# S5 and pooling layer on one core: pooled sums held until the scan is done, pooled maps spread over four output steps, S5 parameters computed among the first channel tiles

## The chip, the cores and the metric

The kernel runs on one core of a Trainium2 chip. The core has a matrix engine (TensorE, PE in the rows; its weight loads are PEld), a vector engine (VectorE, DVE), an activation engine (ScalarE, ACT), a general engine (GpSimd, POOL) and a queue engine that mostly issues transfers (SyncE, SP). Times are device microseconds (us) of one launch; the metric is the median of the runs. The change is called faster or slower by comparing medians of interleaved runs of both kernels.

## The reference

One layer of a diffusion backbone for 128 prompt tokens and 512 sample tokens, width 1024. The part that the change touches is the token mixer:

```
z = h @ w_in + b_in                    # 1024 -> 1024 (u_a) + 512 (u_b) + 2 x 1024 (gates)
s[t] = lam_bar * s[t-1] + b_bar u_a[t] # complex, 64 groups x 64 states, forward and backward
y = Re(C s) + D u_a                    # both directions summed
v = gelu(y); v = v * sigmoid(v @ w_glu + b_glu); ya = v @ w_proj_a
pooled = mean over a window of 2, 4, 8 or 16 tokens (four groups of 128 channels) - u_b
yb = (pooled @ w_pool[group]) * pool_scale @ w_proj_b
out = (sigmoid(g_a) * ya + sigmoid(g_b) * yb) @ w_out + b_out
```

Layer norms with modulation stand before it and after it, and a squared-ReLU MLP of width 4096 follows. Everything is float32; a product of two float32 matrices is made of three passes over parts that are split into a rounded high part and the rest (`split`: ScalarE writes the high part, VectorE the low part).

## The kernel before

Channels lie on the 128 partitions, the 640 tokens along the free axis, in two segments of 320. A weight tile is 128 x 1024 (`wsplit`, L324: one transfer on the SP queue, ACT cast at L321, DVE subtraction at L322); `next_w` (L375) keeps two of them ready ahead of use. The kernel is written as a list of steps; a scheduler fixes, when the kernel is built, the order of instructions on each engine from priorities that follow this list, and semaphores between the engines are all that decides at run time.

- 0 to 60 us: layer norm and modulation (`shift_scale`, L286), the transposed input `hf` (L393 and L394) in eight tiles k, its split `hk` (L396 and L397), and the first two tiles of the input projection (`pu0`, `pu1`) that run along with k. Ahead of the loop over k stands `s5_params(*s5_angles())`: some 80 small VectorE instructions that turn the S5 parameters into tables (`pwt`, `pws`, `pqt`, `pqs`, and the scan's factors `lmr`, `lmi`).
- 60 to 170 us: the other six tiles of u_a (`ua_evac`), and for 16 sets of groups the input matrices of the scan (`gen_in`, `in_proj`), which multiply the tables with `wt` and transpose them on TensorE (L466).
- 170 to 300 us: the scan (`scan_step`, L488): 63 steps of the loop, each of four VectorE instructions (L501 to L504) on 128 x 128, in a chain. Every fourth step a `fill(1)` puts one more tile of the input projection on TensorE (`plain`, L586; the 20 fillers are the pooled branch's input and the gates; 16 of them run before the output steps, 48 matmuls each).
- 255 to 310 us on GpSimd: the pooled sums (`pool_mix`, L654), four groups: a memset of a padded tile `ub` (L656), its transfers (L658), the inverse window counts `ic` (L660), window sums by repeated adds (L667), multiplication and subtraction (L671 and L672). The result is `pls[gi]`.
- 300 to 427 us: 16 output steps e. `out_proj(e)` makes 48 matmuls from the scan's states (`psy`, L574 and L577) and its result goes to DRAM (`yd`, L582) by an ACT copy (L579) and two DVE adds. Beside it, in the steps named at the loop's end (L733 to L746), stand: half a filler tile (`halves`, L596), `pool_map(gi)` (L676: splits `pls[gi]` into `ph`, 6 matmuls, ACT scale, split into `ybx`), `pool_proj(m)` (L687: 24 matmuls on the four `ybx`), and `gelu(m)` (L697: loads `yn` back from `yd`, ACT gelu, split into `vx`).
- from 427 us: the GLU (matmuls on `vx`), the projections, the output projection and the MLP. The change does not touch them.

Of the kernel before, what the change touches and what calls it, by code (L numbers as in the profile page):

```python
# [23 lines left out]
NC = NT // TC  # L24
CP = 16
G = 64
# [12 lines left out]
def hybrid_kernel(ctx: ExitStack, tc: tile.TileContext, xin, cc, w_ada0, w_ada, w_in, w_glu, w_pa, w_pool, w_pb,  # L39
# [35 lines left out]
    def bank(name="ax"):  # L75
        return pp[0].tile([P, 512], F32, tag="ax", bufs=axn[0], name=nm(name))
# [80 lines left out]
    def s5_params(s5t, lr, li, mag, r):  # L157

        pw, tmp = [big0[:, 1280 + 1152 * i:2432 + 1152 * i].rearrange("p (a g k) -> p a g k", a=2, k=9) for i in range(2)]

        def cmul(o, a, b, n):
            ab = [a[i].broadcast_to([P, G, n]) for i in range(2)]
            t0, t1 = tmp[:, 0, :, 0:n], tmp[:, 1, :, 0:n]
            V.tensor_tensor(t0, ab[0], b[0], op=ALU.mult)
            V.tensor_tensor(t1, ab[1], b[1], op=ALU.mult)
            V.tensor_tensor(o[0], t0, t1, op=ALU.subtract)
            V.tensor_tensor(t0, ab[0], b[1], op=ALU.mult)
            V.tensor_tensor(t1, ab[1], b[0], op=ALU.mult)
            V.tensor_tensor(o[1], t0, t1, op=ALU.add)

        nc.gpsimd.memset(pw[:, 0, :, 0:1], 1.0)
        nc.gpsimd.memset(pw[:, 1, :, 0:1], 0.0)
        V.tensor_tensor(pw[:, 0, :, 1], mag, r[:, 0], op=ALU.mult)
        V.tensor_tensor(pw[:, 1, :, 1], mag, r[:, 1], op=ALU.mult)

        def pwr(a, b):
            return [pw[:, i, :, a:b] for i in range(2)]

        cmul(pwr(2, 3), pwr(1, 2), pwr(1, 2), 1)
        cmul(pwr(3, 5), pwr(2, 3), pwr(1, 3), 2)  # L180
        cmul(pwr(5, 9), pwr(4, 5), pwr(1, 5), 4)
        for i in range(2):
            S.copy(lmr[:, i], pw[:, 0, :, 8])
        S.mul(lmi[:, 0], pw[:, 1, :, 8], -1.0)
        S.copy(lmi[:, 1], pw[:, 1, :, 8])
        S.copy(pqt[0:64], pw[0:64, :, :, 1:9])
        S.copy(pqt[64:128], pw[64:128, :, :, 8:0:-1])

        den, dn2, lm1 = s5t([P, G]), s5t([P, G]), s5t([P, G])
        V.tensor_tensor(den, lr, lr, op=ALU.mult)  # L190
        V.tensor_tensor(dn2, li, li, op=ALU.mult)
        V.tensor_tensor(den, den, dn2, op=ALU.add)
        V.reciprocal(den, den)
        V.tensor_scalar(lm1, pw[:, 0, :, 1], -1.0, None, op0=ALU.add)
        cf = half([P, 2, G, 1], "cf")
        a, b = s5t([P, G]), s5t([P, G])
        V.tensor_tensor(a, lm1, lr, op=ALU.mult)
        V.tensor_tensor(b, pw[:, 1, :, 1], li, op=ALU.mult)
        V.tensor_tensor(a, a, b, op=ALU.add)
        V.tensor_tensor(cf[:, 0, :, 0], a, den, op=ALU.mult)  # L200
        V.tensor_tensor(a, pw[:, 1, :, 1], lr, op=ALU.mult)
        V.tensor_tensor(b, lm1, li, op=ALU.mult)
        V.tensor_tensor(a, a, b, op=ALU.subtract)
        V.tensor_tensor(cf[:, 1, :, 0], a, den, op=ALU.mult)
        pc = mat4([P, 2, G, 8], "pc")
        cmul([pc[:, 0], pc[:, 1]], [cf[:, 0], cf[:, 1]], pwr(0, 8), 8)
        S.copy(pwt[0:64], pc[0:64])
        S.copy(pwt[64:128], pc[64:128, :, :, ::-1])
        V.tensor_tensor(pws, pwt[:, 0], pwt[:, 1], op=ALU.add)
        V.tensor_tensor(pqs, pqt[:, 0], pqt[:, 1], op=ALU.add)  # L210
# [75 lines left out]
    def shift_scale(q):  # L286

        ps = bank("psa")
        for k2 in range(4):
            for kk in range(2):  # L290
                for g in range(4):
                    T.matmul(ps[32 * g:32 * g + 32, 0:P], sc[:, 2 * k2 + kk, :], wss[q][k2][:, kk, g, :],
                             start=(k2 + kk == 0), stop=(k2 + kk == 4), skip_group_check=True)
        row = half([P, P], "row")
        S.copy(row, ps[:, 0:P])
        pc = bank("psc")
        T.transpose(pc[:, 0:P], row, ident)
        src = pc[:, 0:P].rearrange("p (m f r) -> p m f r", m=2, f=2)
        for mod in range(2):
            b = colt[:, C_BADA + mod * KT + 2 * q:C_BADA + mod * KT + 2 * q + 2].unsqueeze(2).broadcast_to([P, 2, 2])  # L300
            V.scalar_tensor_tensor(modc[:, mod, 2 * q:2 * q + 2, :], src[:, mod, :, 0:2], float(mod), b,
                                   op0=ALU.add, op1=ALU.add)
# [45 lines left out]
    def tv(t):  # L348
        return t.rearrange("p (n c) -> p n c", n=2)
# [32 lines left out]
    hl0, hl1 = wsplit(w_in[0]), wsplit(w_in[1])  # L382
    wss += [shift_scale_load(q) for q in (1, 2, 3)]
    shift_scale(0)
    s5_params(*s5_angles())
    pu0, pu1 = bank2(), bank2()
    for k in range(KT):
        pa, pb = bank("pst"), bank("pst")
        for t in range(1, NTT):
            T.transpose(pa[:, (t - 1) * P:t * P], xs[t][:, k * P:(k + 1) * P], ident)  # L390
        T.transpose(pb[:, 0:P], xs[0][:, k * P:(k + 1) * P], ident)
        hf = half([P, NT], "hf")
        S.activation(hf[:, P:NT], pa, AF.Identity, scale=modc[:, 1, k, 0:1], bias=modc[:, 0, k, 0:1])  # L393
        S.activation(hf[:, 0:P], pb[:, 0:P], AF.Identity, scale=modc[:, 1, k, 1:2], bias=modc[:, 0, k, 1:2])  # L394
        hk = hslot([P, 2, NT], F32R, "hk")
        V.tensor_copy(hk[:, 0, :], hf)  # L396
        V.tensor_tensor(hk[:, 1, :], hf, hk[:, 0, :].bitcast(F32), op=ALU.subtract)  # L397
        hx.append(hk)
        if k % 2:
            if k < KT - 1:  # L400
                shift_scale(k // 2 + 1)
            for hl, pu in ((hl0, pu0), (hl1, pu1)):
                for kk in (k - 1, k):
                    mm_k(pu, hl, hx[kk], kk, KT, SEG)
# [7 lines left out]
    def state(n):  # L412
        return zt[:, n // 2, :, :, n % 2]
# [237 lines left out]
    E = nc.gpsimd  # L651
    ybx, npp = [], [0]

    def pool_mix(gi):  # L654
        u = pool3([P, 784], "ub")
        E.memset(u, 0.0)  # L656
        for uv, dv in zip(segs_of(u), flat_of(ubd[gi])):
            nc.gpsimd.dma_start(uv, dv)  # L658
        ic = pool2([P, NT], "ic")
        nc.gpsimd.dma_start(ic, invc[gi:gi + 1, :].broadcast_to([P, NT]))  # L660
        yield
        s, lo, hi = u, 0, 784
        for lv in range(gi + 1):
            n = pool3([P, 784], "us")
            d0, d1 = ((1, 0), (1, 1), (2, 2), (4, 4))[lv]
            a, b_ = lo + d0, hi - d1
            E.tensor_tensor(n[:, a:b_], s[:, a - d0:b_ - d0], s[:, a + d1:b_ + d1], op=ALU.add)  # L667
            s, lo, hi = n, a, b_
        p = ic
        for sv, uv, iv in zip(segs_of(s), segs_of(u), flat_of(ic)):  # L670
            E.tensor_tensor(iv, sv, iv, op=ALU.mult)  # L671
            E.tensor_tensor(iv, iv, uv, op=ALU.subtract)  # L672
        pls.append(p)
        yield

    def pool_map(gi, p, wph):  # L676
        ph = hslot([P, 2, NT], F32R, "ph")
        split(p, ph[:, 0, :], ph[:, 1, :])
        ps = bank2()
        mm_k(ps, wph[:, :, gi * P:(gi + 1) * P], ph, 0, 1, SEG)  # L680
        f = gt([P, NT], "yb")
        S.activation(tv(f), v2(ps), AF.Identity, scale=colt[:, C_PSC + gi:C_PSC + gi + 1])
        yb = hslot([P, 2, NT], F32R, "ybx")
        split(f, yb[:, 0, :], yb[:, 1, :])
        ybx.append(yb)
# [20 lines left out]
    for s in range(NC - CP - 1):  # L706
        scan_step(s)
        if s == CP - 1:
            last = s5p.tile([P, 2, 2, G], F32, tag="ta", bufs=2, name="last")[:, 0]
            S.copy(last, state(CP))  # L710
            dma(nstate, last)
            S.copy(state(CP), s0t)
        if s % 11 == 3 and s < 50:
            gen_t(3 + s // 11)
            if s < 40:
                gen_q(4 + s // 11)
        if s % 4 == 0 and s < 60:
            fill(1)
    genctx.close()
    mixctx = ctx.enter_context(ExitStack())  # L720
# [5 lines left out]
    wph = wsplit(w_pool, 512)  # L726
    pls, mixing = [], [pool_mix(gi) for gi in range(4)]
# [5 lines left out]
    for e in range(16):  # L733
        out_proj(e)
        if e + 4 < 16:
            load_out(e + 4)
        if e < 8:
            next(part)
        if e in (6, 7):
            for gi in (2 * e - 12, 2 * e - 11):  # L740
                pool_map(gi, pls[gi], wph)
        if e in (8, 9, 10, 11, 12, 13, 15):
            pool_proj(npp[0])
            npp[0] += 1
        if e % 2 and e > 4:
            gelu(e // 2 - 2)  # L746
# [136 lines left out]
    for t in range(NTT):  # L883
# [18 lines left out]
        for h in range(2):  # L902
            pt = bank("pst")
            for i in range(4):
                k = 4 * h + i
                T.transpose(pt[:, i * P:(i + 1) * P], tmp[:, k * P:(k + 1) * P], ident)
            for i in range(4):
                k = 4 * h + i
# [143 lines left out]
    for qf in range(3):  # L1052
# [12 lines left out]
        for fh in range(2):  # L1065
            pa, pb, pc_ = bank2(), bank2(), bank("ps4")
            pt = [pa[:, 0], pa[:, 1], pb[:, 0], pb[:, 1], pc_]
            for kp in range(4):
# [4 lines left out]
                for kk in range(2):  # L1073
                    k = 2 * kp + kk
# [125 lines left out]
```

## Time and profile before

| | us |
|---|---|
| runs | 1068.2, 1066.11, 1066.76; median 1066.76 |
| the profiled execution's own time | 1064.7 |
| its span | 1062.9 |
| mean granted TensorE clock | 0.977 of full speed |
| busy: PE, DVE, ACT, POOL | 986.3, 706.7, 400.4, 108.1 |

The span is the time from the first to the last instruction; the execution's own time is 1.8 us longer. TensorE is busy for 93% of the span. In the page's row of tenths over 40 slices (each 26.6 us), PE shows a 4 and a 6 in the tenth to thirteenth slices, `9469`, where all later slices are full, and the granted clock shows `769` in about the same place. That is the end of the scan.

### The profile page before, as it was taken

The page shows a single profiled execution, that of the slowest core. Times are in us where ns is not written, and L with a number is a line of the kernel's source. Part 1 is how long each engine was busy: PE and PEld are TensorE (multiplying, and loading weights), DVE is VectorE, ACT ScalarE, POOL GpSimd, SP SyncE. Part 2 cuts the span into 40 slices and gives each one's busy share as a digit, 9 for nine tenths or more (in the row PEclk, how much of TensorE's full clock was granted, in tenths as well). Part 3 has the DMA queues.
Part 4 walks back from the last instruction along what each step waited for, and adds up shares of the span by engine and source line. Part 5 has one row for each costly group of instructions (what it writes and reads, how often), then busy time and mean ns, then how long its engine had stood idle before and what let it go on. Part 6 is the DMA issues. An engine that isn't in the chain of part 4 may idle for free.

```text
span 1062.9 us, 18300 instructions
## 1 busy us (share of the span) xinstructions
PE 986.3 (93%) x7464; PEld 894.0 (84%) x7464; DVE 706.7 (66%) x1163; ACT 400.4 (38%) x667; POOL 108.1 (10%) x148
## 2 busy tenths in 40 slices
PE   3899998999469799999999999989999999999997
PEld 2798887998469798999987899868998899889876
DVE  8977768999931233544856874579864586358676
ACT  5546554332101443532222544313651266116610
POOL 0222321201760000200000000000000000000000
PEclk9999999999769899999999999999999999999999
DMA  9676767856447588977753044523221222212421
GB/s 357 191 211 191 190 195 229 246 169 180 119 131 216 148 248 268 335 253 248 250 182 118 1 139 139 145 63 99 81 93 66 80 80 99 76 63 81 158 80 60
DMA packets 117116, 166.84 MB, mean 157 GB/s; under 512 B 47848, under 2 KB 80616, under 8 KB 117032
## 3 DMA queue, kind: packets, MB, share of 16 engines
q1 hardware_dynamic: 111656, 146.27, 43.9%
q0 software_dynamic: 5376, 19.40, 5.2%
q8 instruction: 59, 0.97, 0.4%
q14 instruction: 25, 0.20, 0.1%
HBM read 135.30 MB, written 30.34 MB: 156 GB/s over the span
## 4 chain that ended last, share of the span: by engine, by line
PE 60%; DVE 14%; DMA 12%; issue 6%; ACT 4%; POOL 3%; SPq 1%; DVEq 0%; ACTq 0%; POOLq 0%
PE ps L336 20%; PE ps L1077 13%; PE ps L1010 8%; PE psx L1010 6%; PE pse L1100 3%; PE ps L890 2%; PE psy L574 2%; DMA wr<-in_w_in_dram 2%; DVE wh L322 2%; DMA wa<-in_w_ada_dram 1%; PE psa L236 1%; PE psz L480 1%; DMA wr<-in_w_out_dram 1%; PE ps L1100 1%; DVE zt L504 1%
## 5 line engine op out<-in xcount | busy, mean ns | idle before, releaser
L336 PE MATMUL ps<-hk,wh 128*128 128x320 f32 x1344 | 214.6, 317 | 9.5 <-DVE hk L396 4.4
L336 PEld LDWEIGHTS ps<-hk,wh 128*128 128x128 f32 x1344 | 202.0, 192 | 15.9 <-DVE hk L396 5.4
L322 DVE TENSOR_TENSOR wh<-wr,wh 128x1024 fp32r<-128x1024 f32 (+1 forms) x113 | 130.1, 1152 | 105.9 <-ACT wh L321 104.9
L321 ACT CAST wh<-wr 128x1024 fp32r<-128x1024 f32 (+1 forms) x113 | 109.4, 968 | 170.1 <-PE ps L1077 84.9
L1077 PE MATMUL ps<-wh,fx 128*128 128x512 f32 x720 | 166.4, 392 | 3.7 <-DVE wh L322 2.3
L1077 PEld LDWEIGHTS ps<-wh,fx 128*128 128x128 f32 x720 | 135.9, 189 | 32.7 <-DVE wh L322 2.7
L574 PE MATMUL psy<-zt,q 64*128 64x80 f32 x512 | 43.9, 285 | 21.9 <-POOL us L667 21.9
L336 PEld LDWEIGHTS ps<-gx,wh 128*128 128x128 f32 x384 | 56.4, 187 | 3.3 <-issue 2.9
L336 PE MATMUL ps<-gx,wh 128*128 128x320 f32 x384 | 58.7, 310 | 0.0
L574 PEld LDWEIGHTS psy<-zt,q 64*128 64x128 f32 x512 | 37.1, 199 | 25.5 <-POOL us L667 22.1
L336 PEld LDWEIGHTS ps<-vx,wh 128*128 128x128 f32 x384 | 56.4, 188 | 2.5 <-ACT sg L817 2.1
L336 PE MATMUL ps<-vx,wh 128*128 128x320 f32 x384 | 58.1, 311 | 0.0
L224 POOL DMA_DIRECT2D wa<-in_w_ada_dram x32 | 16.9, 533 | 342.9 <-DVE vx L322 124.0
L1010 PE MATMUL psx<-h,wh 128*128 128x320 f32 x288 | 47.5, 308 | 0.0
L1010 PE MATMUL ps<-h,w 128*128 128x320 f32 x288 | 46.5, 307 | 0.0
L1010 PEld LDWEIGHTS psx<-h,wh 128*128 128x128 f32 x288 | 43.7, 187 | 0.2
L1010 PEld LDWEIGHTS ps<-h,w 128*128 128x128 f32 x288 | 43.2, 187 | 0.0
L855 DVE TENSOR_TENSOR ps<-ps,gate 128x512 f32<-128x512 f32 (+2 forms) x39 | 28.1, 748 | 17.9 <-PE ps L1077 12.9
L589 ACT ACTIVATE g<-ps,colt 128x640 f32<-128x640 f32 x16 | 12.7, 795 | 65.5 <-PE ps L336 65.5
L890 PE MATMUL ps<-wo,mx 128*128 128x512 f32 x150 | 36.6, 392 | 0.7 <-ACT wo L321 0.6
L890 PEld LDWEIGHTS ps<-wo,mx 128*128 128x128 f32 x150 | 27.9, 188 | 7.2 <-ACT wo L321 1.5
L336 PE MATMUL ps<-ybx,wh 128*128 128x320 f32 x192 | 31.6, 321 | 2.6 <-ACT wh L321 2.6
(264 smaller groups left out, 1666.3 us busy)
## 6 DMA issues: line engine op xcount, KB each, us to landing
wr<-in_w_m_dram SPq DMA_DIRECT2D x64, 512.0 KB, 3.9
wa<-in_w_ada_dram POOLq DMA_DIRECT2D x32, 512.0 KB, 5.2
wr<-in_w_in_dram SPq DMA_DIRECT2D x28, 512.0 KB, 5.0
qd<-q SPq DMA_DIRECT2D x8, 1024.0 KB
q<-qd SPq DMA_DIRECT2D x16, 512.0 KB, 5.5
x<-in_xin_dram SPq DMA_DIRECT2D x10, 512.0 KB, 7.5
wa<-in_w_ada_dram SPq DMA_DIRECT2D x10, 512.0 KB, 9.2
tm<-sd SPq DMA_DIRECT2D x8, 512.0 KB
```

What stands on the lines that cost most here:

```text
L224: nc.gpsimd.dma_start(w, w_ada[self.mod, :, k * D:(k + 1) * D])
L236: T.matmul(self.ps[32 * q:32 * q + 32, 0:256], sc[:, k, :], w[:, q * 256:(q + 1) * 256], start=(k == 0), stop=(k == KT - 1), skip_group_ch ...
L321: S.copy(hi, raw)
L322: V.tensor_tensor(lo, raw, hi.bitcast(F32), op=ALU.subtract)
L336: T.matmul(ps[:, n, 0:ln], hl[:, wh, k * P:(k + 1) * P], xk[:, xh, o:o + ln], start=(k == 0 and i == 0), stop=(k == nk - 1 and i == 2))
L574: T.matmul(o, q[d, l, i, :], zt[d, 0:NC // 2, i, 4 * e + l, :], start=(i == 0), stop=False, skip_group_check=True)
L589: S.activation(tv(g), v2(ps), func, bias=colt[:, C_BIN + m:C_BIN + m + 1])
L855: V.tensor_tensor(ps, ps, g[:, c0:c1], op=ALU.mult)
L890: T.matmul(ps[:, n, :], mx[k][:, xh, t * P:(t + 1) * P], wo[k][:, wh, n * 512:(n + 1) * 512], start=(k == 0 and i == 0), stop=(k == KT - 1 ...
L1010: T.matmul(ps, hl[:, wh, c + k * P:c + (k + 1) * P], rq[b][:, xh, k, :], start=(start and k == 0 and i == 0), stop=(stop and k == 3 and i ...
L1077: T.matmul(pt[t], fx[k][:, xh, t * P:(t + 1) * P], hl[:, wh, kk * 512:(kk + 1) * 512], start=(k == 0 and i == 0), stop=(k == 7 and i == 2))
L1100: T.matmul(ps[n][:, 0:ln], fx[k][:, xh, t * P:(t + 1) * P], hl[:, wh, o_:o_ + ln], start=(k == 0 and i == 0), stop=(k == 7 and i == 2))
```

## The change

Four edits. The S5 parameters, computed before the loop over the channel tiles k, are now computed inside it, `s5_angles` at k = 1 and `s5_params` at k = 5. GpSimd copies the scan's last state (`state(NC - 1)`) into the first pooling tile ahead of that tile's memset, which overwrites it. One more filler tile is put into the scan (17 in place of 16), and two fewer half steps run beside the output steps (6 in place of 8). The four pooled maps run in output steps 5, 6, 7 and 8, one each (before: two in step 6 and two in step 7), and the pooled projections in steps 9 to 15 (before: 8 to 13 and 15).

```
-    s5_params(*s5_angles())
     pu0, pu1 = bank2(), bank2()
     for k in range(KT):
...
         if k % 2:
             if k < KT - 1:
                 shift_scale(k // 2 + 1)
+            if k == 1:
+                ang = s5_angles()
+            if k == 5:
+                s5_params(*ang)
...
     def pool_mix(gi):
         u = pool3([P, 784], "ub")
+        if gi == 0:
+            E.tensor_copy(u[:, 0:2 * G].rearrange("p (a g) -> p a g", a=2), state(NC - 1))
         E.memset(u, 0.0)
...
-        if s % 4 == 0 and s < 60:
+        if s % 4 == 0 and s < 61:
             fill(1)
...
         out_proj(e)
         if e + 4 < 16:
             load_out(e + 4)
-        if e < 8:
+        if e < 6:
             next(part)
-        if e in (6, 7):
-            for gi in (2 * e - 12, 2 * e - 11):
-                pool_map(gi, pls[gi], wph)
-        if e in (8, 9, 10, 11, 12, 13, 15):
+        if 5 <= e < 9:
+            pool_map(e - 5, pls[e - 5], wph)
+        if e > 8:
             pool_proj(npp[0])
             npp[0] += 1
```

GpSimd's queue, at the start of the pooled sums. Before, the memset and the transfers of the first two groups, then the first add (`us`):

```order
L656 MEMSET ub_3622 128x784
L660 DMA ic_3626<-in_invc_dram 128x640
L658 DMA ub_3622<-ubd 128x128
L658 DMA ub_3622<-ubd 128x8x64
L656 MEMSET ub_3628 128x784
L660 DMA ic_3632<-in_invc_dram 128x640
L658 DMA ub_3628<-ubd 128x128
L658 DMA ub_3628<-ubd 128x8x64
L667 TENSOR_TENSOR us_3634<-ub_3622 128x783
```

The same place in the changed kernel, where lines after the edit are five higher and `zt` is the tile of the scan's states:

```order
L665 DMA ic_3684<-in_invc_dram 128x640
L665 DMA ic_3690<-in_invc_dram 128x640
L665 DMA ic_3702<-in_invc_dram 128x640
L665 DMA ic_3716<-in_invc_dram 128x640
L660 COPY ub_3679<-zt 128x128
L661 MEMSET ub_3686 128x784
L661 MEMSET ub_3679 128x784
L663 DMA ub_3686<-ubd 128x128
L663 DMA ub_3679<-ubd 128x128
L663 DMA ub_3679<-ubd 128x8x64
L663 DMA ub_3686<-ubd 128x8x64
L672 TENSOR_TENSOR us_3692<-ub_3679 128x783
```

The copy from `zt` stands ahead of both memsets, of the transfers of `ub` and of all sums; only the transfers of the four `ic` stand ahead of it.

VectorE's queue at the end of the loop over k (`hk_620` and `hk_633` are the last two channel tiles, `wh_697` the weights of the first tile after the pair `pu0`, `pu1`). Before:

```order
L434 TENSOR_TENSOR q_683<-oy_689,q_683 128x8x128
L438 TENSOR_TENSOR q_683<-q_683,oy_689 128x8x128
L322 TENSOR_TENSOR wh_697<-wr_696,wh_697 128x1024
L431 TENSOR_TENSOR oy_767<-pws,b_762 128x512
L396 CAST hk_620<-hf_617 128x640
L432 TENSOR_TENSOR wt_766<-pwt,b_762 128x4x128
L397 TENSOR_TENSOR hk_620<-hf_617,hk_620 128x640
L396 CAST hk_633<-hf_630 128x640
L433 TENSOR_TENSOR wt_766<-pwt,b_762 128x4x128
L397 TENSOR_TENSOR hk_633<-hf_630,hk_633 128x640
```

The same place in the changed kernel:

```order
L395 CAST hk_620<-hf_617 128x640
L167 TENSOR_TENSOR big_96<-cf_566,big_96 128x64x8
L168 TENSOR_TENSOR big_96<-cf_566,big_96 128x64x8
L396 TENSOR_TENSOR hk_620<-hf_617,hk_620 128x640
L169 TENSOR_TENSOR pc_575<-big_96 128x512
L395 CAST hk_633<-hf_630 128x640
L436 TENSOR_TENSOR q_683<-pqt,c_680 128x8x128
L396 TENSOR_TENSOR hk_633<-hf_630,hk_633 128x640
L209 TENSOR_TENSOR pws<-pwt 128x512
L437 TENSOR_TENSOR q_683<-oy_689,q_683 128x8x128
L441 TENSOR_TENSOR q_683<-q_683,oy_689 128x8x128
L322 TENSOR_TENSOR wh_697<-wr_696,wh_697 128x1024
```

The last two channel tiles now stand ahead of the table `pws` and of `wh_697`, and the first set of input matrices (`wt_766`, which needs `pws`) stands behind `wh_697`.

ScalarE's queue around the second pooled map, in the changed kernel (`ph` is a pooled sum's high part, `yn` the reloaded output and `vf` its gelu, `g` the gate of a filler tile):

```order
L609 ACTIVATE g_4125<-ps_4040,colt 128x640
L321 CAST wh_4432<-wr_4431 128x512
L687 ACTIVATE yb_4138<-ps_4131,colt 128x640
L321 CAST ybx_4140<-yb_4138 128x640
L582 COPY y_4150<-psy_4151 128x320
L706 ACT_TABLE_LOAD
L706 ACTIVATE vf_4145<-yn_4143 128x640
L321 CAST vx_4147<-vf_4145 128x640
L321 CAST ph_4188<-ic_3690 128x640
L582 COPY y_4203<-psy_4204 128x320
```

The cast of the second pooled sum stands behind the first gelu, and the third and fourth follow it.

## Rows read from the trace of the kernel before

**Rows 1.** Stretches of time (first two columns), engines' busy time and counts, granted clock.

```profile
60.00:170.00 110.00, 104.60 (x1279) 94.50 (x1277) 80.47 (x106) 63.96 (x164) 30.53 (x48) 1.00 0.70 195
170.00:272.20 102.20, 98.04 (x888) 95.75 (x885) 97.25 (x266) 30.36 (x58) 15.55 (x13) 1.00 0.67 201
278.80:300.70 21.90, 0.03 (x1) 0.02 (x1) 21.59 (x23) 1.84 (x2) 21.53 (x23) 0.55 0.27 85
300.70:427.20 126.50, 118.07 (x1177) 111.94 (x1178) 34.43 (x64) 42.00 (x59) 9.05 (x7) 0.93 0.71 215
```

**Rows 2.** Waits between 240 and 312 us: total, times, longest.

```profile
PE psy L574 <- POOL us L667: 21.9, 1, 21.9
```

**Rows 3.** TensorE in order of time around the scan's end: start, duration, work.

```profile
264.51 14.32 PE L336 MATMUL ps<-hk,wh 128*128 128x320 f32 x96 [0.93 <-ACT g L589]
...
300.71 1.15 PE L574 MATMUL psy<-zt,q 64*128 64x80 f32 x8 [21.88 <-POOL us L667]
...
306.05 4.83 PE L336 MATMUL ps<-hk,wh 128*128 128x320 f32 x24
310.81 0.68 PE L574 MATMUL psy<-zt,q 64*128 64x80 f32 x8
...
313.65 3.78 PE L336 MATMUL ps<-hk,wh 128*128 128x320 f32 x24
317.36 0.67 PE L574 MATMUL psy<-zt,q 64*128 64x80 f32 x8
```

**Rows 4.** VectorE in order of time, 255 to 276 us.

```profile
255.19 1.22 DVE L322 TENSOR_TENSOR wh<-wr,wh 128x1024 fp32r<-128x1024 f32 x1
...
257.37 0.29 DVE L501 TENSOR_TENSOR ta<-lmr,zt 128x128 f32<-128x128 f32 x1
...
258.43 0.29 DVE L501 TENSOR_TENSOR ta<-lmr,zt 128x128 f32<-128x128 f32 x1
...
272.22 3.58 DVE L322 TENSOR_TENSOR wh<-wr,wh 128x1024 fp32r<-128x1024 f32 x1
```

**Rows 5.** VectorE's groups from 275.7 to 300.6 us: busy, mean ns, idle before.

```profile
L504 DVE TENSOR_TENSOR zt<-ta,tb 128x128 f32<-128x128 f32 x6 | 7.3, 1222 | 0.2
L322 DVE TENSOR_TENSOR wh<-wr,wh 128x1024 fp32r<-128x1024 f32 (+1 forms) x3 | 6.5, 2180 | 0.0
```

**Rows 6.** GpSimd in order of time, 200 to 310 us.

```profile
205.80 4.92 POOL L513 TENSOR_TENSOR c<-c 128x128 f32<-128x128 f32 x1 [8.37 <-DMA c<-in_cpk_dram]
218.50 0.46 POOL L518 TENSOR_TENSOR c<-c 128x128 f32<-128x128 f32 x1 [7.78 <-ACT q L517]
...
257.81 1.44 POOL L658 DMA_DIRECT2D ub<-ubd  x2
...
273.21 1.50 POOL L667 TENSOR_TENSOR us<-ub 128x783 f32<-128x783 f32 x1
...
308.26 1.72 POOL L672 TENSOR_TENSOR ic<-ic,ub 128x128 f32<-128x128 f32 x2
```

**Rows 7.** VectorE in order of time, the loop over k.

```profile
37.92 0.69 DVE L209 TENSOR_TENSOR pws<-pwt 128x512 f32<-128x512 f32 x1 [2.24 <-ACT pwt L208]
...
56.01 0.81 DVE L397 TENSOR_TENSOR hk<-hf,hk 128x640 fp32r<-128x640 f32 x1
```

**Rows 8.** TensorE in order of time, start of the first tile after the pair.

```profile
60.14 7.30 PE L336 MATMUL ps<-hk,wh 128*128 128x320 f32 x48
```

**Rows 9.** TensorE's waits from 340 to 427.2 us: total, times, longest.

```profile
PE ps L336 <- ACT ph L321: 5.8, 3, 4.9
PE ps L336 <- ACT wh L321: 2.6, 1, 2.6
```

**Rows 10.** ScalarE in order of time, before the first pooled map.

```profile
343.67 0.79 ACT L606 ACTIVATE g<-ps,colt 128x640 f32<-128x640 f32 x1 [3.25 <-PE ps L336]
...
352.98 1.28 ACT L701 ACT_TABLE_LOAD   x1 [6.01 <-DMA yn<-yd]
...
356.21 0.72 ACT L321 CAST ph<-ic 128x640 fp32r<-128x640 f32 x1
```

More of the change, by code (lines that the diff above doesn't have):

```diff
@@ L384, in hybrid_kernel @@
     shift_scale(0)
-    s5_params(*s5_angles())
     pu0, pu1 = bank2(), bank2()
@@ L401, in hybrid_kernel @@
                 shift_scale(k // 2 + 1)
+            if k == 1:
+                ang = s5_angles()
+            if k == 5:
+                s5_params(*ang)
             for hl, pu in ((hl0, pu0), (hl1, pu1)):
@@ L655, in pool_mix @@
         u = pool3([P, 784], "ub")
+        if gi == 0:
+            E.tensor_copy(u[:, 0:2 * G].rearrange("p (a g) -> p a g", a=2), state(NC - 1))
         E.memset(u, 0.0)
@@ L716, in hybrid_kernel @@
                 gen_q(4 + s // 11)
-        if s % 4 == 0 and s < 60:
+        if s % 4 == 0 and s < 61:
             fill(1)
@@ L736, in hybrid_kernel @@
             load_out(e + 4)
-        if e < 8:
+        if e < 6:
             next(part)
[L739 to L742, printed above, removed]
+        if 5 <= e < 9:
+            pool_map(e - 5, pls[e - 5], wph)
+        if e > 8:
             pool_proj(npp[0])
```

## The prediction

> **What bounds the kernel now.** I read the engines' busy time by stretches first, since TensorE's 93% is an average. From 60 to 170 us TensorE is busy 104.6 of 110 us and VectorE has 29 us to spare; in the scan (170 to 272.2) TensorE has 98 of 102 and VectorE 97; in the output steps TensorE has 118 of 126.5. Between 278.8 and 300.7, TensorE does nothing (0.03 us), while VectorE (21.59) and GpSimd (21.53) are busy without a break [rows 1]. That is the only large hole, and the list of waits has it as one wait of 21.9 us at the first output matmul [rows 2, 3]. It names GpSimd's adds, but these write `us`, which the matmul doesn't read; it reads the states `zt`. What ends last there is the scan itself, whose last instruction ends at 300.6, so I look at the scan's own pace.
>
> Up to 272.2 a scan step takes 1.06 us (from one first multiplication to the next) with instructions of 0.29 [rows 4]. GpSimd's first add of the pooled sums begins at 273.21 [rows 6]. From then on the same adds of the scan take 1222 ns on average, and the weight splits 2180 in place of 1220 [rows 4, 5], the one that overlaps the first add even 3.58. Six steps and three splits fill 272.2 to 300.6; nothing of the scan waits for any other engine there (idle before: 0.2). The scan's data and shapes have not changed, only GpSimd's work beside it has. So TensorE waits for the scan, and the scan is held up by GpSimd.
>
> **The pooled sums behind the scan (A).** The copy from `zt` holds GpSimd's memsets, transfers and sums until the last step is done. Then the rest of the scan runs at its own pace: 272.2 + one split of 1.22 + six steps of 1.06 = 279.8, in place of 300.6; two of the three splits stand behind the last step in the changed order, and these delay nobody on TensorE for the next 6 us. TensorE's sixteenth filler ends at 278.8, and the new seventeenth takes half of the 14.32 us that two take [rows 3], 7.2, so the first output matmul comes at 286.2 with some 0.2 between; by then the scan has been over for 6 us. That is 14.5 us sooner, and the seventeenth filler is missing later: two half steps of 3.71 each (313.65 to 317.36) go [rows 3]. 14.5 + 7.4 = 21.9, the whole wait. Bounds: 0 if the pace isn't GpSimd's doing (a rival below), 21.9 above.
>
> The price: GpSimd's chain, from 273.2 to 310 before (37 us, of which some held it up) [rows 6], now begins after the scan. A copy and two memsets, at most the 1.50 of an add each, and four transfers at 0.72 put the first add some 7 us after the scan's end, and the last result some 35 us later, at 279.8 + 7 + 35 = 322. The first map needs only the first sum, after the sixth half step: 286.2 + 6 x 6.55 (the period of steps, 310.81 to 317.36) = 325.5. The fourth is needed about 25 us later. So I cost it at nothing, with the output steps as its cover; if it were late, maps would wait by the microsecond.
>
> A rule speaks against it. With GpSimd beside it, a VectorE instruction on two operands waits about as long as one of GpSimd's adds lasts (0.29 us becomes 1.2; the add is 1.50) [rows 4 to 6], and earlier in the scan it was GpSimd that was held up: one 128x128 add took 4.92 where a like one took 0.46 [rows 6]. The Trainium skill (page "SBUF — State Buffer", section "Who interferes with whom") has both: VectorE instructions with two inputs in SBUF and GpSimd instructions that read it exclude each other, and whoever issued first goes on. By that rule the lock is moved, not removed: the weight splits of the output steps meet it. By the row, each split would take 2.2 to 3.6 in place of 1.2; some ten of them cost 10 to 24 us of VectorE, which is busy only 34 of 126.5 there [rows 1], and splits run ahead by two tiles. Either way the sum stays.
>
> **The clock (B).** In the hole the granted clock is 0.55, and 0.93 over the output steps [rows 1]. The first output step took 5.34 us (300.71 to 306.05) and its half tile 4.76, where the second took 2.84 and 3.71 [rows 3]: 2.5 + 1.1 = 3.6 us were lost to a clock that came back late. TensorE, busy without a break to 286 now, should keep it: -3.6 (between 0 and -3.6).
>
> **The S5 parameters (C).** In the loop over k VectorE is the engine that is late: TensorE starts the first tile after the pair at 60.14 [rows 8], some 3 us behind VectorE's last channel split (56.82) [rows 7]. In the changed order that split stands ahead of `pws`, two table instructions and the next weights; the three instructions of the first `wt` (0.69 each, by `pws` of the same shape) and two scan instructions (0.7) go behind the weights, and the stall of 2.24 before `pws`, for ScalarE, may go [rows 7]. The weights, behind which the next tile now stands, then end at 56.8 - 2.1 - 0.7 - 2.2 = 51.8 at best, or 54 without the last term. Against that stands new waiting, as the parameters' small instructions now depend on ScalarE and GpSimd between the tiles; the one row of such a wait is the 2.24, and I allow one or two (2 to 4.5). So the tile starts at 54 to 58.5 instead of 60.1; I take 57: -3. The first tables, now later (about 62 against 58), are wanted by TensorE only after the tile, at 64. From 60 to 170 TensorE is the bound and in the scan it has 4 us of slack, so the shift carries on. Bounds: -5, and +2 where four such waits come.
>
> **The output steps (D).** Before, TensorE waits there 5.8 us in three waits for the casts `ph` and 2.6 for a projection's weights, 8.4 [rows 9]. The 4.9 is the first map behind the first gelu: the gate at 343.67, its store, the load of `yn`, a table load at 352.98, gelu, casts, `ph` at 356.93: 13.4 us after the half tile ended [rows 10]. Now the first map comes before the gelu, but the second stands behind it, with the same gate ahead. TensorE has the first map (0.9), two output steps (2 x 2.84) and part of a third (1.1) to do meanwhile, 7.7: it waits 13.4 - 7.7 = 5.7. The fourth map stands behind the second gelu, whose load is issued after step 8's result is stored: 1.4 (copy, adds, issue) + a load, 6.0 by the idle time before the first gelu [rows 10], + 2.7 (gelu and two casts) = 10.1, against 2 1/4 output steps and a map (7.3): 2.8. With 0.4 for the rest, 8.9. Removed 8.4, added 8.9: +0.5. Ends: -8.4 (all gone) and +6 (both loads as slow as 8, and a projection's weights late as before).
>
> **The sum.** Against the profiled execution's 1064.7: -21.9 - 3.6 - 3.0 + 0.5 = -28.0, 1036.7. The median of the runs lies 2.1 above that execution, so 1038.8: 1039 us.
>
> **The rivals.** *The ScalarE queue (20%).* More of the output steps hang on gelu: every `yn` load stands in front of something that TensorE wants, weight casts of the projections too. For it: the chain of 13.4 us and the 2.6 for weights [rows 9, 10]. Against it: from step 9 on TensorE has 24 projection matmuls per step to hide a load. Price: the fourth map at 4.9 in place of 2.8, and three waits of 2.6, together 10: 1049.
>
> *The early edit turns against itself (10%).* The split parameters put more dependent waits into the loop, and the scan starts up to 5 us later, not 3 sooner: +8, 1047. For it: VectorE has no slack there. Against: the late instructions leave its queue in front of the channel splits.
>
> *The gate doesn't do what it says (4%).* If the scan's end slowed down for another reason (its own splits, the transfers), it still ends at 300.6 and only the filler fits in the hole: -7.4, and about -3 with C: 1057. Against it: the pace changes within a microsecond of GpSimd's first add, and splits of 1.22 fit between steps of 1.06 before [rows 4, 6].
>
> *Slower: GpSimd becomes the one that is late (4%).* If VectorE's adds hold it up as they held `c`, 4.92 for 0.46, each of its 26 adds, products and differences costs up to 4.5 us more: 117 us if always. The fourth map is wanted some 62 us after the first add can start. At a share of half, the chain takes 35 + 58 = 93 and TensorE waits 31, more than the gain: 1070; that half is the point from which it decides. Against it: VectorE is busy 27% of the output steps [rows 1], which gives 67 us, 5 late.
>
> **How the numbers follow.** The forecast has 62%, the four rivals 38%. A measurement of this kernel can tell 0.2%, 2 us, from no change: only the last rival, and a mixture of two others, reach that. Faster 0.94, same 0.02, slower 0.04. The range: below, C at -5 and D at -4 give 1032.5, rounded to 1031; above, the first two rivals end at 1049 and 1047, and both in part at 1053. Some 3% lie below and 10% above.
>
> **What would show it.** Right: the scan's four instructions stay at about 290 ns to the last, its end lies at 275 to 280, the first output matmul (283 with C) has no wait, its step takes 2.8 and the granted clock stays at full from 270 on. GpSimd's first `us` begins after the scan's end and the last result is there by 320, with no wait of `ph` on GpSimd. The first tile after the pair starts at about 57. The maps' waits for ScalarE sum to 8 to 9, and the GLU starts near 399 (427.2 before). Wrong: scan instructions of 1 us with GpSimd silent; a hole before the first output matmul; maps that wait for GpSimd; or output steps that last over 120 us between the first output matmul and the GLU.

## The result and the profile after

The changed kernel takes 1047.71 us (median of four runs, 1047.18 to 1049.21), the kernel before 1066.43 in the same comparison: a ratio of 0.9824, 95% interval 0.9807 to 0.9841, so 18.7 us faster. Forecast were 1039 in a range of 1031 to 1053. The direction and the main cause came out; the gain is 9 us short, and one step of the sum had the wrong sign. The profiled execution took 1047.25 us (17.45 less than that of before), its span is 1045.5.

The stretches of the changed kernel, with the columns of [rows 1]:

```profile
60.00:170.00 110.00, 100.52 (x1120) 90.30 (x1120) 79.90 (x107) 58.42 (x146) 37.44 (x45) 0.95 0.68 192
278.80:300.70 21.90, 21.90 (x197) 21.43 (x198) 10.65 (x31) 4.77 (x7) 11.28 (x14) 1.00 0.74 232
292.30:409.00 116.70, 112.64 (x1130) 107.32 (x1130) 36.01 (x63) 39.55 (x57) 34.61 (x32) 0.90 0.81 234
342.60:366.00 23.40, 23.39 (x162) 21.49 (x163) 6.90 (x15) 7.77 (x13) 0.00 (x0) 0.50 0.66 166
```

The hole is gone: from 278.8 to 300.7 TensorE, idle in [rows 1], is busy for all 21.9 us at full clock. Two new things show. From 60 to 170 TensorE is busy 100.5 us where it was 104.6, at 0.95 of the clock. And the output steps hold 23.4 us at a granted clock of 0.50, the lower of the two levels.

VectorE's groups in the scan's last 23 us (line numbers here are three higher; the first is the last instruction of each scan step), to be held against [rows 5]:

```profile
L507 DVE TENSOR_TENSOR zt<-ta,tb 128x128 f32<-128x128 f32 x20 | 5.9, 293 | 0.7
...
L322 DVE TENSOR_TENSOR wh<-wr,wh 128x1024 fp32r<-128x1024 f32 x4 | 4.9, 1218 | 0.0
```

The scan keeps 293 ns (1222 before) and the split 1218 (2180) to the end. GpSimd in order of time, against [rows 6]:

```profile
103.50 6.53 POOL L459 TENSOR_TENSOR b<-b 128x64 f32<-128x64 f32 x1 [6.08 <-DVE wt L437]
110.11 0.83 POOL L460 TENSOR_TENSOR b<-b 128x64 f32<-128x64 f32 x1
110.90 0.46 POOL L516 TENSOR_TENSOR c<-c 128x128 f32<-128x128 f32 x1
111.31 0.75 POOL L369 COPY ujr<-uj 128x128 f32<-128x128 f32 x1
112.00 1.07 POOL L370 COPY ujr<-uj 128x512 f32<-128x512 f32 x1
...
286.28 1.22 POOL L660 COPY ub<-zt 128x128 f32<-128x128 f32 x1 [7.04 <-DVE zt L507]
...
295.25 1.54 POOL L672 TENSOR_TENSOR us<-ub 128x783 f32<-128x783 f32 x1 [3.58 <-DMA ub<-ubd]
...
328.81 1.72 POOL L677 TENSOR_TENSOR ic<-ic,ub 128x128 f32<-128x128 f32 x2
```

The gate holds: the copy runs 0.1 us after the scan's last step, and the last sum is there at 330.5, in time for every map. The first row is the surprise. A 128x64 add, 0.3 to 1.2 us elsewhere, lasted 6.53 us, and the reversed copies of u stand behind it. What follows is seen on SP and on TensorE:

```profile
113.10 0.37 SPq L371 DMA_DIRECT2D urd<-ujr  x1
113.56 0.53 SPq L451 DMA_DIRECT2D u<-ud  x1
```

```profile
57.60 7.30 PE L336 MATMUL ps<-hk,wh 128*128 128x320 f32 x48 [0.72 <-ACT uj L364]
...
117.30 0.77 PE L483 MATMUL psz<-u,w 128*64 128x80 f32 x4 [5.71 <-DMA u<-ud]
...
271.06 21.36 PE L336 MATMUL ps<-hk,wh 128*128 128x320 f32 x144 [0.93 <-ACT g L592]
292.35 0.68 PE L577 MATMUL psy<-zt,q 64*128 64x80 f32 x8
...
295.19 3.78 PE L336 MATMUL ps<-hk,wh 128*128 128x320 f32 x24
...
333.26 0.61 PE L577 MATMUL psy<-zt,q 64*128 64x80 f32 x8
333.71 0.39 PE L580 MATMUL psy<-u,tm 64*128 64x80 f32 x4
333.93 0.61 PE L577 MATMUL psy<-zt,q 64*128 64x80 f32 x8
...
342.61 0.74 PE L336 MATMUL ps<-ph,wh 128*128 128x320 f32 x2 [3.38 <-ACT ph L321]
...
347.07 1.06 PE L577 MATMUL psy<-zt,q 64*128 64x80 f32 x8
347.93 0.63 PE L580 MATMUL psy<-u,tm 64*128 64x80 f32 x4
348.35 1.06 PE L577 MATMUL psy<-zt,q 64*128 64x80 f32 x8
...
408.99 14.24 PE L336 MATMUL ps<-vx,wh 128*128 128x320 f32 x96
```

The first tile after the pair starts 2.5 us sooner (57.60; 60.14 in [rows 8]). At 117.30 TensorE has waited 5.7 us for u, and from there the whole kernel runs late: the last three fillers start at 271.06 and take 7.1 each, so that the second of them, the sixteenth, ends at 285.3 (278.8 in [rows 3]). So the first output matmul follows without a wait, but 9 us later than the 283 of the forecast. A quarter of an output step takes 0.67 us (333.26 to 333.93) ahead of the 3.4 us wait, and 1.28 (347.07 to 348.35) behind it.

### The profile page after: what moved, and what is told of

The parts are those of the page before. It is cut to its first block, busy times and chain, and to the rows that moved or that the text cites. A ratio compares the mean times of both kernels' runs of the same rounds, so it can differ in the third digit from the quotient of the medians.

```text
span 1045.5 us, 18289 instructions
## 1 busy us (share of the span) xinstructions
PE 991.3 (95%) x7464; PEld 897.7 (86%) x7464; DVE 691.4 (66%) x1163; ACT 398.0 (38%) x665; POOL 114.4 (11%) x149
## 4 chain that ended last, share of the span: by engine, by line
PE 72%; DMA 10%; DVE 6%; issue 5%; ACT 4%; POOL 1%; SPq 1%; DVEq 0%; POOLq 0%; ACTq 0%
PE ps L336 28%; PE ps L1081 13%; PE ps L1014 8%; PE psx L1014 6%; PE ps L894 4%; PE pse L1104 3%; DMA wa<-in_w_ada_dram 3%; PE psy L577 2%; PE psa L236 1%; PE psz L483 1%; PE ps L1104 1%; PE psy L580 1%; PE pst L469 1%; DMA gate<-grd 1%; DMA wr<-in_w_out_dram 1%
## 5 line engine op out<-in xcount | busy, mean ns | idle before, releaser
L577 PE MATMUL psy<-zt,q 64*128 64x80 f32 x512 | 46.3, 299 | 0.0
L577 PEld LDWEIGHTS psy<-zt,q 64*128 64x128 f32 x512 | 39.6, 213 | 3.3 <-issue 3.3
L483 PE MATMUL psz<-u,w 128*64 128x80 f32 x512 | 27.4, 250 | 7.7 <-DMA u<-ud 7.7
L483 PEld LDWEIGHTS psz<-u,w 128*64 128x64 f32 x512 | 23.2, 146 | 12.5 <-issue 9.5
```

What stands on the lines that cost most here:

```text
L483: T.matmul(ps[64 * d:64 * d + 64, o:o + NC], w[:, 2 * h + l, r, 64 * d:64 * d + 64], us[m][d][:, (e % 2) * 4 + 2 * h + l, :], start=True, ...
L577: T.matmul(o, q[d, l, i, :], zt[d, 0:NC // 2, i, 4 * e + l, :], start=(i == 0), stop=False, skip_group_check=True)
```

## The experiments

Theory: the gate (the copy of the scan's last state, for which GpSimd has to wait) gives the whole gain, because GpSimd's reads of the memory that VectorE uses hold up the scan (G); and the missing 9 us went to the one long add, which VectorE held off, the other way round (L). The rivals are with each run. Each kernel's ratio to the kernel before, from interleaved runs, is given with its interval.

**The S5 parameters back ahead of the loop.** The changed kernel with that edit undone (the removed line stands again, the four added ones go).

> The changed kernel with one edit undone: the S5 parameters are computed ahead of the loop over k again. Theory L (lockout): in the changed kernel one add of 128x64 on GpSimd lasted 6.53 us (103.5 to 110) while VectorE ran two-operand instructions without a break, the reversed copies of u behind it came late, TensorE waited 5.7 us for u, and the start of the scan moved from 3 us sooner to 6.4 us later; with the old order the add falls elsewhere. Then the third tile's wait for u is under 1 us, the first output matmul comes at about 286 (292.4 with the edit) and the time is 1041 us. Rival T (the transfer is late by itself, or the other edits shift the channel tiles): a wait of 5 us for u stays, first output matmul at 292, 1047.5 us.

Measured 1041.79 us, ratio 0.9787 (0.9755 to 0.9818), within a microsecond of the forecast of L; its four runs (1041.0 to 1042.9) all lie under the changed kernel's (1047.2 to 1049.2). TensorE's rows in order of time:

```profile
112.56 0.46 PE L480 MATMUL psz<-u,w 128*64 128x80 f32 x4 [0.89 <-DMA u<-ud]
...
286.51 0.68 PE L574 MATMUL psy<-zt,q 64*128 64x80 f32 x8
```

and GpSimd's small add, which stands in the same place of its queue as the long one did:

```profile
98.14 0.58 POOL L456 TENSOR_TENSOR b<-b 128x64 f32<-128x64 f32 x1 [0.86 <-DMA b<-in_bpk_dram]
```

**The S5 parameters alone.** The kernel before with only that edit:

```
-    s5_params(*s5_angles())
...
+            if k == 1:
+                ang = s5_angles()
+            if k == 5:
+                s5_params(*ang)
```

> The kernel before with only the S5 parameters moved into the loop over k. Theory L: the first tile after the pair starts some 2.5 us sooner, the wait of 5 to 6 us for u appears near 112, the last input matrices come 6 us later than before, and the whole kernel is slower: 1072 us (1069 to 1074). Rival S (the early edit is good, and the 6 us come from elsewhere): 1063 to 1066 us.

Measured 1070.85, ratio 1.0051 (1.0023 to 1.0080): slower, as L has it. The first tile after the pair starts at 56.7, and then come the same long add and the same wait:

```profile
102.93 6.51 POOL L459 TENSOR_TENSOR b<-b 128x64 f32<-128x64 f32 x1 [6.09 <-DMA b<-in_bpk_dram]
```

```profile
116.87 0.76 PE L483 MATMUL psz<-u,w 128*64 128x80 f32 x4 [5.87 <-DMA u<-ud]
...
305.93 1.14 PE L577 MATMUL psy<-zt,q 64*128 64x80 f32 x8 [21.86 <-POOL us L670]
```

The hole of 21.9 us has its old length and lies 5.2 us later: what the channel tiles lose goes straight to the end.

**The gate alone.** The kernel before with the copy only:

```
         u = pool3([P, 784], "ub")
+        if gi == 0:
+            E.tensor_copy(u[:, 0:2 * G].rearrange("p (a g) -> p a g", a=2), state(NC - 1))
         E.memset(u, 0.0)
```

> The kernel before with only the copy of the scan's last state ahead of the pooled sums. Theory G (GpSimd's sums slow the scan): every scan instruction takes 0.28 to 0.30 us to the end, the scan ends near 280, the first output matmul starts there without the clock's fall, 21 us sooner, and another 3.6 us come from the clock: 1042 us. The other edits then bring under 3 us together. Rival F (the scan's end is slow for another reason, the gain is the filler in the hole): the last steps stay at 1 us per instruction, 1066 us.

Measured 1042.05 (1039.07 to 1047.43), ratio 0.9794 (0.9749 to 0.9838). The scan keeps its pace to the end:

```profile
L504 DVE TENSOR_TENSOR zt<-ta,tb 128x128 f32<-128x128 f32 x20 | 5.9, 293 | 0.7
```

and the first output matmul comes at 282.98, 17.7 us sooner. The 21 of the expectation were not reached: this execution's channel tiles ended 1.2 us later than before's, and its scan at 282.9 and not near 280. So one copy is worth all that the four edits bring together without the early one (1041.8). By the medians it is also worth 5.7 us more than all four, but there the intervals (0.9749 to 0.9838 and 0.9807 to 0.9841) overlap; that the early edit costs time is shown by the run before this one.

**All but the gate.** The changed kernel without the copy.

> The changed kernel without the copy of the scan's last state, so that the pooled sums run beside the scan again; the other three edits stay. Theory G: the scan's last steps take 1 us per instruction again and end at about 307 (300.6 before, and 6.4 later because of the early edit), the seventeenth filler ends at 292.4, a hole of 15 us and a slow clock behind it (3.6): 1066 us (1062 to 1068). Rival F (the other edits carry the gain): 1047 to 1052 us.

Measured 1063.38, ratio 0.9971 (0.9947 to 0.9995), within G's range. VectorE's groups from 275.7 to 303:

```profile
L507 DVE TENSOR_TENSOR zt<-ta,tb 128x128 f32<-128x128 f32 x8 | 10.0, 1246 | 0.3
```

```profile
303.40 1.14 PE L577 MATMUL psy<-zt,q 64*128 64x80 f32 x8 [12.71 <-POOL ic L675]
```

The slow scan is back, 1246 ns, and with it a hole of 12.7 us (15 expected). The long add is there too, 6.53 us at 103.05, with a wait of 6.0 us for u. The other three edits together gain 3 us, the added filler among them.

**Memsets in place of the sums.** The kernel before; the place and the time of GpSimd's work stay, but nothing of it reads the memory.

```
-            E.tensor_tensor(n[:, a:b_], s[:, a - d0:b_ - d0], s[:, a + d1:b_ + d1], op=ALU.add)
+            for _ in range(2):
+                E.memset(n[:, a:b_], 0.0)
...
-            E.tensor_tensor(iv, sv, iv, op=ALU.mult)
-            E.tensor_tensor(iv, iv, uv, op=ALU.subtract)
+            for _ in range(4):
+                E.memset(iv, 0.0)
```

> The kernel before with each add, product and difference of GpSimd's pooled sums replaced by two memsets of the same shape, at the same place and of about the same duration; the pooled branch is left out by that, everything else stays. Theory R (GpSimd's reads hold the scan up): the scan keeps 0.29 us per instruction beside the memsets, ends near 280, and the time is as with the sums held back: 1042 us (1039 to 1045). Rival A (any work of GpSimd on the same memory holds the scan up): instructions of about 1 us, a hole near 20 us before the first output matmul, 1066 us.

Measured 1044.52, ratio 0.9805 (0.9768 to 0.9841). VectorE from 274.4 to 282, while GpSimd, busy for all of these 7.6 us, writes tiles of 128x783, 128x512 and 128x128 between its transfers:

```profile
L504 DVE TENSOR_TENSOR zt<-ta,tb 128x128 f32<-128x128 f32 x6 | 1.7, 292 | 0.2
```

The scan does not notice the writes, so it was GpSimd's reads that held it up. This is what the Trainium skill states (page "SBUF — State Buffer", section "Who interferes with whom"): a VectorE instruction with two inputs in SBUF contends with a GpSimd instruction that reads SBUF, not with one that only writes it. The runs agree: 1222 ns beside the sums, 292 beside memsets.

**The small adds on VectorE.** The changed kernel with the two small instructions on b for each set of input matrices moved:

```
-        nc.gpsimd.tensor_tensor(b[:, :, 2, :], b[:, :, 0, :], b[:, :, 1, :], op=ALU.add)
-        nc.gpsimd.tensor_tensor(b[:, :, 1, :], b[:, :, 1, :], b[:, :, 0, :], op=ALU.subtract)
+        V.tensor_tensor(b[:, :, 2, :], b[:, :, 0, :], b[:, :, 1, :], op=ALU.add)
+        V.tensor_tensor(b[:, :, 1, :], b[:, :, 1, :], b[:, :, 0, :], op=ALU.subtract)
```

> The changed kernel with the 32 small adds and subtractions on b (two for each set of input matrices) on VectorE in place of GpSimd. Theory L: nothing long stands before the reversed copies of u, the wait for u at 112 is under 1.5 us, the start of the scan keeps the 2.5 us of the early edit, and the first output matmul comes at about 284: 1039 us (1037 to 1042); the adds cost VectorE about 6 us of the 29 it has to spare there. Rival T (the transfer is late by itself): 1047 us.

Measured 1038.80, ratio 0.9767 (0.9731 to 0.9802). TensorE's waits from 60 to 170 us:

```profile
PE psz L483 <- DMA u<-ud: 2.1, 1, 2.1
```

The 5.7 us wait is gone with the long add (the 2.1 is another, at 139, which the other kernels have between 141 and 147). VectorE pays 5.5 us more of busy time there (85.4 against 79.9) and has it to spare. The first output matmul comes at 286.0, not at 284: of the early edit's 2.5 us little arrives there, and whether the 3 us to the kernel with the old place of the S5 parameters are real can't be told, as the intervals overlap. Four kernels that are the same up to there (that of before and the runs with the old place and the gate, the memsets or all other edits) end their channel tiles between 168.7 and 170.9 us, the changed kernel at 176.1 and this one at 168.0: the loss stands clear of that spread, the gain does not. No run took away VectorE's work beside the long add. That the add made the kernel late is shown; that VectorE held it is read from their overlap (last section).

**The maps' cast on VectorE.** In the changed kernel the second map waits 3.4 us on ScalarE behind a gelu, and the half clock follows.

```
-        split(p, ph[:, 0, :], ph[:, 1, :])
+        V.tensor_copy(ph[:, 0, :], p)
+        V.tensor_tensor(ph[:, 1, :], p, ph[:, 0, :].bitcast(F32), op=ALU.subtract)
```

> The changed kernel with the high part of the pooled sums (the cast into ph) written by VectorE in place of ScalarE, so that a pooled map no longer stands behind a gelu. In the changed kernel TensorE waited 3.4 us for the second map's cast, and the granted clock was 0.50 for the 23.4 us behind that wait. Theory C (the wait also costs the clock): the wait goes, the clock stays at 1.00 through the maps, and besides the 3.7 us hole some 11 us of half clock are saved: 1033 us (1031 to 1036). Rival W (only the wait counts; the slow stretch is slow for its own reasons): 1044 us. Rival M (the wait comes back at the next map, behind the first map's results on ScalarE): 1047 us.

Measured 1045.47, ratio 0.9815 (0.9788 to 0.9842). The time lies between rivals W and M, and the trace shows M (the wait comes back at the next map). The second map no longer waits, the third does, and the engine named is VectorE, whose queue now holds the third cast behind the low part of the first gelu:

```profile
346.06 0.90 PE L336 MATMUL ps<-ph,wh 128*128 128x320 f32 x2 [3.47 <-DVE ph L683]
```

**Both mends.**

> The changed kernel with both mends: the small adds on b on VectorE, and the high part of the pooled sums on VectorE. If both causes are right they add up: 1038.8 less 14.7: 1024 us (1022 to 1028), with the first output matmul at 286 and the GLU at 388. If the second mend only takes its wait away: 1035 us. If the two are one and the same (a slower channel part only moves the maps): 1033 us or more.

Measured 1036.23, ratio 0.9728 (0.9701 to 0.9755): the 1024 us of two mends that add up were missed. The time fits both other lines, and as its interval overlaps that of the small adds alone, it is not shown that the second mend brings anything. The wait at the third map is 2.5 us, and 340 to 350 runs at a clock of 0.50. By its median it is the fastest version of all, 11 us below the changed kernel.

**Gelus behind the maps.** Alone, and with the small adds on VectorE:

```
-        if e % 2 and e > 4:
-            gelu(e // 2 - 2)
+        if e > 8:
+            gelu(e - 9)
```

> The changed kernel with only the gelus moved behind the pooled maps. The wait for u near 112 and the later scan stay (first output matmul at 292.4). Theory C: 3.4 us of wait and 11 us of slow clock go: 1033 us (1031 to 1037). Rival W: 1044 us. Rival Q: 1041 to 1047 us.

> The changed kernel with the small adds on b on VectorE, and with the gelus moved behind the pooled maps: one each in output steps 9 to 15 (before: one each in 5, 7, 9, 11, 13 and 15, and the seventh behind). No pooled map then stands behind a gelu on any engine. Theory C (a short wait costs the clock far more than itself): no wait of ph, granted clock 1.00 from the first output matmul to the GLU, 3.8 us of wait and 10 to 11 us of slow clock less than with the small adds alone: 1025 us (1023 to 1029). Rival W (the slow stretch has another cause): 1035 us. Rival Q (seven gelus in seven steps make the weight casts of the projections late on ScalarE, and the wait comes back there): 1032 to 1038 us.

Measured 1045.73, ratio 0.9803 (0.9776 to 0.9830), and 1038.71, ratio 0.9749 (0.9712 to 0.9785): rival Q in both (the wait comes back at a projection), in the second 0.7 us above its range. Stretches of the second kernel, whose profiled execution was the fastest of its four (1034.52):

```profile
326.00:350.00 24.00, 23.85 (x288) 22.23 (x290) 8.49 (x19) 11.32 (x17) 0.00 (x0) 1.00 0.84 235
350.00:370.00 20.00, 16.08 (x197) 15.30 (x194) 5.74 (x11) 5.43 (x8) 0.00 (x0) 1.00 0.92 256
370.00:395.00 25.00, 21.80 (x164) 20.37 (x165) 10.09 (x18) 10.73 (x15) 0.00 (x0) 0.86 0.74 228
```

```profile
373.13 1.43 PE L336 MATMUL ps<-ybx,wh 128*128 128x320 f32 x4 [6.42 <-ACT wh L321]
```

The maps run at full clock without a wait worth naming, as theory C of these expectations has it, and the wait comes back, longer, at the fifth projection: its weights' transfer is issued on SP only at 369.48, behind stores and loads that wait, and the cast, itself behind two gelus, starts when that transfer lands. The output steps, from the first output matmul to the GLU, take 112.1 us here and 111.4 in the other, against 116.6; part of these 5 us is lost again in the GLU, whose inputs come later.

**Gelus in steps 8, 10, 11, 13, 14 and 15**, with the small adds on VectorE.

> As the kernel with late gelus and the small adds on VectorE, but the gelus in output steps 8, 10, 11, 13, 14 and 15 (the seventh and eighth behind), so that a projection's weight transfer is no longer queued behind two gelu loads. Theory Q (the wait of 6.4 us for a projection's weights was the price of one gelu per step): that wait falls under 2 us, no wait of ph comes back, the granted clock stays at 1.00 through the maps, and the time is 1029 us (1025 to 1033). Rival: the four shared buffers of 128 x 640 or the weight tiles set the pace whatever the order, and a wait of 4 to 7 us shows at another projection: 1035 to 1039 us.

Measured 1041.34, ratio 0.9758 (0.9726 to 0.9790): a miss, above the theory's range and the rival's. The fifth projection waits as long as before, with the gelus elsewhere:

```profile
373.84 6.51 PE L336 MATMUL ps<-ybx,wh 128*128 128x320 f32 x24 [6.64 <-ACT wh L321]
```

What holds that transfer back, the shared 128 x 640 buffers or the two raw weight tiles, was not taken apart.

## Why the prediction was partly right

**A, the pooled sums behind the scan: right.** With the gate the scan keeps 293 ns to the end, without it 1246, with it alone the gain is 24 us; the memsets show that the reads did it. The first output matmul, corrected for the later fillers, comes where the sum put it: 278.8 + 6.5 + 7.1 = 292.4. GpSimd's chain took 44 us from the scan's end and not 42, and no map waited for it. Of the three splits on VectorE beside it two were held up, as the prediction allowed for: 1.82 and 2.03 us (at 319.99 and 323.37) where these shapes take 0.69 and 0.82 elsewhere; TensorE did not wait behind them.

**B, the clock: right at its place.** The first output step takes 2.84 us (292.35 to 295.19; 5.34 before), and the clock is 1.00 from 278.8 until the wait at 339.

**C, the S5 parameters: wrong, and this is the whole miss.** The step that failed is "From 60 to 170 TensorE is the bound and in the scan it has 4 us of slack, so the shift carries on". The tile did start 2.5 us sooner (3 forecast). But the shift of the queues let one small add on GpSimd fall into a stretch in which VectorE ran two-operand instructions back to back, and it was held for 6.5 us; the copies of u behind it, the transfer behind these and TensorE behind the transfer came late, and the fillers ended 6.5 us later: +6.5 in place of -3, 9.5 us off. Of the 9 us between the tile's 2.5 sooner and the fillers' 6.5 later, 4.9 are the longer wait (5.71 against 0.85 for the same tile before), and about 3, an estimate, the clock behind it, 0.88 from 118 to 130 us and 0.96 from there to 170, where it was 1.00 before; the rest was not taken apart. The rival "The early edit turns against itself" had the sign and the time (1047), with another mechanism. That VectorE can hold up GpSimd was on the table, with the row of an add that took 4.92 us [rows 6], and it was weighed only for the output steps; the stretch with the most two-operand work beside GpSimd's, 80 and 31 us of busy time [rows 1], was not asked.

**D, the output steps: right in size, by other terms.** Forecast +0.5, measured 116.6 - (126.5 - 7.4 - 3.6) = +1.1. But the waits are 4.1 us (3.4 and 0.7) and not 8.9: the second map's 13.4 us chain was 11 (its gelu's load came sooner), and the fourth map had no wait. In their place stands the half clock behind the 3.4 us: 0.6 us on each of some eleven quarters of output steps, and 0.9 on each of three maps (0.90 and 1.43 in place of 0.56 and 0.85), nearly 10 us. It probably hid the fourth map's chain as well: the cast for that map ended at 359.35, and TensorE came to the map only at 362.65. The old stage had such a stretch too, 9 us at 0.67 behind its wait of 4.9. I had counted a clock only at the old hole, and not behind the waits that I forecast myself.

**The sum as measured**: -21.9 - 3.6 + 6.5 + 1.1 = -17.9 to the GLU (408.99 against 427.19: -18.2), and 0.8 is lost behind it; between the two profiled executions lie 17.45. The rival in which GpSimd becomes late in the output steps did not come about there; its mechanism came in the channel tiles, on one instruction.

## What to carry to other kernels

Work on GpSimd that reads the on-chip memory is not free beside a dependent chain of small two-operand VectorE instructions: look for their mean duration before and after GpSimd starts, and order the two engines by a true dependence if it doubles. If an edit shifts an engine's queue by a few microseconds, look at every short GpSimd instruction in front of a transfer within the shifted stretch, and ask what VectorE does at that moment. A wait of 3 us on TensorE can cost 13 if the clock falls behind it, so a wait that you forecast needs a clock term too; and where one queue hides several loads, a wait that is removed in one place is likely to turn up at the next.

## What the runs showed of the hardware that was not expected

Who holds up whom is not symmetric. At the scan's end (instructions of 0.29 us in a chain) about half of VectorE's instructions waited, each for about one GpSimd instruction, and GpSimd was hardly slowed: its add took 1.50 us beside the scan [rows 6] and 1.54 after it (295.25). In the channel tiles it was GpSimd that got nothing. From 103.50 to 109.85 VectorE ran eight more instructions without a gap (each started before the one ahead of it had ended), and the add ended in the first gap, 0.2 us in which VectorE itself waited for it:

```profile
109.16 0.69 DVE L434 TENSOR_TENSOR oy<-pws,b 128x512 f32<-128x512 f32 x1
110.07 0.69 DVE L435 TENSOR_TENSOR wt<-pwt,b 128x512 f32<-128x512 f32 x1 [0.21 <-POOL b L459]
```

The add of 4.92 us in the kernel before fits this. It began at 205.80, earlier in the scan, where weight splits and 128x256 steps also ran without a gap, and it ended at 210.72, after the first gap: VectorE's instruction at 210.12 ended at 210.41, and the next, at 210.44, took 0.43 in place of 0.29. At the scan's end such gaps of 0.03 to 0.04 us come twice a step (270.92 to 270.95 and 271.24 to 271.28). So GpSimd seems to get in where VectorE leaves a gap, and VectorE then waits for GpSimd's instruction. That is a reading of these rows, which no run tested, and two rows of the kernel with the S5 parameters back ahead speak against it: a 128x64 add at 98.14 took 0.58 and a 128x128 add at 105.72 took 0.73, beside VectorE work that was nearly as dense.

The granted clock fell to 0.50 behind a wait of 3.4 us and stayed there for 23 us of unbroken work on output steps and maps, but was 0.86 on average over the 25 us in which a wait of 6.4 us stood among the large projections. The length of the wait does not give the price; what it was that did was not tested.
